# Portions of projection work dealt out anew between eight attention head pairs, with three pairs' closing transposes on other PSUM tiles

## The chip, the cores and the metric

The kernel runs on one NeuronCore of a Trainium2 chip. TensorE (PE) multiplies matrices and writes its results to PSUM; VectorE (DVE) and ScalarE (ACT) read PSUM, do the elementwise work and write to SBUF; GpSimd (POOL) does small elementwise work out of SBUF; SyncE (SP) issues most of the DMA transfers. Each engine works through its own list of instructions in order, and semaphores hold an instruction back until what it needs is there.

The metric is the device time in microseconds (us) of one launch of the whole program. The time before is the median of three runs, 1453.44 us (1450.69 to 1454.27). All times of single steps come from one profiled execution.

## The reference

One inference step of a two-layer encoder for 512 prompt frames and 8 running streams of 16 new frames, all in float32, model width 1024, 16 heads of 64. Layer 0 is a convolution module with an FFN. Then one K and one V are projected, and layer 1 projects queries and attends. Cut to the attention part, which is where the change lies:

```
k, v = split(rms_norm(h, norm_kv) @ w_kv, 2)
q = (rms_norm(h, norm_attn) @ w_q)             # 16 heads of 64
s = einsum("bqhd,bkhd->bhqk", q, k) * Dh**-0.5 + bias
p = softmax(where(valid, s, -1e30))
o = einsum("bhqk,bkhd->bqhd", p, v)
h = h + o @ w_o
h = h + (silu(a) * b) @ w_out                  # a, b from rms_norm(h) @ w_in
```

The prompt attends to itself in chunks of 64 frames, the running streams attend to 512 cached rows of K and V beside their own 16. A learned bias by head and clipped distance is added.

## The kernel before, in words

Activations lie with the feature on the partitions: `h` is 128 x 8 x 640, where 640 columns are 128 sample frames and 512 prompt frames. A float32 product is made of three fast matmuls: each operand is split into a high and a low part (ACT rounds the high part, DVE subtracts it to get the low part), and high x high, low x high and high x low are summed in PSUM. Splitting weights and activations is the main work of ACT and DVE.

The program has three stretches: layer 0, the attention, and the FFN of layer 1 with the final norm. The attention goes over eight pairs of heads, `p` = 0 to 7. Two kinds of work are woven into one PE order there:

- **Pair steps**, small and full of waits. `A` (`heads`, `head_a`): the prompt's scores, 24 matmuls, then bias, maximum, exp and scale on DVE and ACT. `s0`, `s1` (`samp_a`): scores of the running streams, two halves. `b00` to `b12` (`head_b`): transposes of the prompt's softmax rows, for two heads in three portions. `t0`, `t1` (`samp_b`): transposes of the streams' rows; `n0`, `n1` (its `rest`): one more transpose each, of the columns of the new frames, which DVE copies into `PM` and `PN`. `c0`, `c1` (`samp_c`): the streams' products with V, which DVE then scales into `Sn` and `Ss` (L1522). `P` (`pair_c`): the prompt's product with V, split by `osplit` into `oT[p]`. `d0`, `d1` (the `rest` of `samp_c`, L1524): one transpose each of the scaled rows and two `osplit`s of its halves.
- **Filler** (`stream`): the projections that the next pairs need, cut into portions of a few matmuls, in the order of `SETS`: `k` sets (K and Q of one pair, 12 portions), `v` sets (V of two pairs, 15 portions) and `o` sets (the output projection of two pairs, 16 portions, `set_o`). k1 and v1 come in pair 0, k2 in pair 1, and so on; o2 is the last. Each set also emits the splitting of the next set's weights (`pieces`), tied by `behind` to the last softmax instructions noted in `past`.

`BO[p]` is the order of pair p written out: a letter for a step, `f4` for four portions of filler, `f*` for what is left of the pair's portions. `FILL[p]` is the number of portions that pair p takes. Every PE instruction of a step is issued behind the one before (`pe`, `step_end`), so PE's order is exactly this text: if a step waits, PE waits. The steps have high priority over all later work; within that, the tile framework fixes each engine's order by its own simulated timeline. An instruction that comes early in ACT's or DVE's list is done first even if something more urgent becomes ready behind it.

PSUM has eight banks, three pools of tiles here: two `w2` tiles of two banks each (`w2t`: scores of `A`, of `s0` and `s1`, and, if `spare_w2[0]` is set, two portions of an `o` set side by side, evacuated by one wide add, L1361), two `am` tiles of one bank (`amt`: the last part of the scores in `A`, and the steps b, t, n, c, P and d) and two `mm` tiles of one bank (`mmt`: the filler). A tile can be written again when its readers are done. `spare_w2[0]` is cleared at `A` and set right after `s1`; `set_o` takes a `w2` tile for an even portion while more than two portions of the pair are left.

After pair 7 come `halves(3)`: the last quarter of the output projection, whose weights are split by `wsplit` (L178 on ACT, L183 on DVE, 128 x 2048 in one instruction each) as soon as the weight tile of the set two before it is free, which is at the end of k7, in pair 6. It takes `mm` and `am` tiles in turn and needs `oT[6]` and `oT[7]` whole. Then layer 1's FFN starts, with PE as the busy engine.

Of the kernel before, what the change touches and what calls it, by code (L numbers as in the profile page):

```python
# [15 lines left out]
P = 128  # L16
# [5 lines left out]
NP = H // 2  # L22
# [40 lines left out]
HIX = {X11: 0, X21: 1, XT1: 2, XT2: 3, XT3: 4, X22: 5, XT4: 6}  # L63
QORD = """50' a0 a1 10' 50" 10" 20 60' 30' 51' 60" 30" 51" 70 11 21 40 61 31 52 71 12 22 41 62 32 53 72
          13 23 42 63 33"""
BO = ["A f4 s0 s1 f3 b00 f1 b01 f1 b02 f1 b10 f1 b11 f1 b12 f1 t0 f1 t1 f1 n0 f1 n1 f1 c0 c1 P f1 d0 f1 d1 f*"] * 8
BO[1] = BO[6] = "A f4 s0 s1 f3 b00 f1 b01 b02 f1 b10 f1 b11 b12 f1 t0 t1 f1 n0 n1 c0 c1 P d0 d1 f*"
BO[7] = "A f2 s0 s1 f5 b00 f1 b01 b02 f1 b10 f1 b11 b12 f1 t0 f1 t1 n0 n1 f1 c0 c1 P d0 f1 d1 f*"
FILL = 27, 12, 28, 27, 28, 27, 12, 16
SETS = "k1 v1 k2 k3 o0 k4 v2 k5 o1 k6 v3 k7 o2"  # L70
LAG = 1
SSQ1 = 'aaaaaaaa'
# [13 lines left out]
def tile_trunk(ctx, tc, xT, vecs, hist, w_pw1, w_pw2, w_in0, w_out0, w_os0, w_in1, w_out1, w_os1,  # L86
# [17 lines left out]
    def nm(s):  # L104
        uid[0] += 1
        return f"{s}_{uid[0]}"
# [1017 lines left out]
    def amt():  # L1124
        return am.tile([P, 512], F32, tag="am", name=nm("am"))
# [29 lines left out]
    def bias_load(p):  # L1155
        for hh in range(2):
            hd = 2 * p + hh
            nc.sync.dma_start(BP[:, hh, 256:512],
                              bass.AP(tensor=rel.tensor, offset=rel.offset + hd * L + 127,
                                      ap=[[RELW - 1, P], [1, 256]]))  # L1160
            nc.gpsimd.tensor_scalar(out=BP[:, hh, 256:512], in0=BP[:, hh, 256:512],
                                    scalar1=t256[:, hd:hd + 1], scalar2=8.0,
                                    op0=ALU.subtract, op1=ALU.mult)
            nc.gpsimd.memset(BP[0:64, hh, 448:512], NEG)
        bt = ap.tile([P, 160], F32, tag="bt", name=nm("bt"), bufs=1)
        for b in range(4):
            nc.sync.dma_start(bt[b * 32:(b + 1) * 32, 0:128],
                              bass.AP(tensor=rel.tensor, offset=rel.offset + 2 * p * L + 127,
                                      ap=[[L, 2], [RELW - 1, 16], [1, 128]]))
            nc.sync.dma_start(bt[b * 32:(b + 1) * 32, 128:144],  # L1170
                              bass.AP(tensor=rel.tensor, offset=rel.offset + 2 * p * L + 255,
                                      ap=[[L, 2], [RELW - 1, 16], [1, 16]]))
        nc.gpsimd.tensor_scalar(out=BS[:, 384:512], in0=bt[:, 0:128], scalar1=ts_[:, p:p + 1],
                                scalar2=8.0, op0=ALU.subtract, op1=ALU.mult)
        for b in range(4):
            nc.gpsimd.tensor_scalar(out=BS[b * 32:(b + 1) * 32, 512 + b * 16:528 + b * 16],
                                    in0=bt[b * 32:(b + 1) * 32, 128:144],
                                    scalar1=ts_[b * 32:(b + 1) * 32, p:p + 1],
                                    scalar2=8.0, op0=ALU.subtract, op1=ALU.mult)
# [26 lines left out]
    fill, step_end, spare_w2 = None, [None], [None, []]  # L1206
    ahead, past, left = {}, [{}] * LAG, [0]

    def note(ins):
        ahead[ins.ins.engine] = ins.ins  # L1210
        return ins

    def osplit(src, hi, lo):
        note(xsplit(src, hi, lo))
        ahead[split_end[0].engine] = split_end[0]
# [47 lines left out]
    @contextmanager  # L1263
    def pe():
        with tc.issue_after(step_end[0]) if step_end[0] else nullcontext():
            yield
# [134 lines left out]
    def heads(ts):  # L1401
        KH, KL, QH, QL = ts
        wide = [w2t(), w2t()]
        narrow = [amt(), amt()]
        pss = [[], []]
        for i in ORD:
            n = (i + 1) * P
            o = SOFF[i]
            q = slice(i * P, (i + 1) * P)
            for hh in range(2):  # L1410
                pss[hh].append(narrow[hh][:, 0:n] if i == 1 else wide[hh][:, o:o + n])
            for j, (a, b) in enumerate(((QH, KH), (QL, KH), (QH, KL))):
                for hh in range(2):
                    r = slice(hh * DH, hh * DH + DH)
                    with pe():
                        step_end[0] = nc.tensor.matmul(pss[hh][-1], a[r, q], b[r, 0:n],
                                                       start=j == 0, stop=j == 2).ins
        return pss
# [47 lines left out]
    def samp_load(p, u):  # L1466
        cache = []
        for src in (kc[p, u], vc[p, u].rearrange("p b k d -> p b (k d)")):
            for i in range(2):
                t = ap.tile([P, 2, 512], F32, tag="cache", name=nm("cache"), bufs=CB)  # L1470
                nc.sync.dma_start(t, src[:, 2 * i:2 * i + 2, :])
                cache.append(t)
        return cache[:2], cache[2:]
# [35 lines left out]
    def samp_c(p, u, PTs, S, rs, VC):  # L1509
        v0 = 64 * u  # L1510
        PT, pn = PTs
        VT = vts[p // 2]
        pv = amt()
        for k in range(5):
            for b in range(4):
                c = slice(k * P + 32 * b, k * P + 32 * b + 32)
                step_end[0] = nc.tensor.matmul(
                    pv[32 * b:32 * b + 32, 0:P], PT[:, c] if k < 4 else pn[:, 32 * b:32 * b + 32],
                    VC[b // 2][:, b % 2, k * P:(k + 1) * P] if k < 4
                    else VT[:, 0, (p % 2) * P:(p % 2) * P + P], start=k == 0, stop=k == 4).ins  # L1520
        os_ = S[:, 0:P]
        note(nc.vector.tensor_scalar(out=os_, in0=pv[:, 0:P], scalar1=rs[:, 0:1], scalar2=None,  # L1522
                                     op0=ALU.mult))
        def rest():  # L1524
            tr = amt()
            step_end[0] = nc.tensor.transpose(tr[:, 0:P], os_, ident).ins
            trv = tr[:, 0:P].rearrange("p (b h q) -> p b h q", b=4, h=2)
            for hh in range(2):
                r = slice(hh * DH, hh * DH + DH)
                osplit(trv[r, :, hh, :],  # L1530
                       oT[p][0][r, v0:v0 + 64].rearrange("p (b q) -> p b q", q=SB),
                       oT[p][1][r, v0:v0 + 64].rearrange("p (b q) -> p b q", q=SB))

        return rest
# [24 lines left out]
    for p in range(NP):  # L1559
        if p < NP - 1:  # L1560
            oT[p] = (op_.tile([P, NT], F32R, tag="ohi", name=nm("ohi"), bufs=3),
                     op_.tile([P, NT], F32R, tag="olo", name=nm("olo"), bufs=3))
        else:
            oT[p] = (op_.tile([P, NT], F32, tag="kt", name=nm("ohi"), bufs=2).bitcast(F32R),
                     op_.tile([P, NT], F32, tag="qt", name=nm("olo"), bufs=QB).bitcast(F32R))
        ha, sa, pt, ps, left[0] = {}, {}, {}, {}, FILL[p]
        cache = [samp_load(p, u) for u in range(2)]
        for op in BO[p].split():
            if op[0] == "f":
                for _ in range(left[0] if op[1] == "*" else min(left[0], int(op[1]))):  # L1570
                    with pe():
                        next(fill)
                    left[0] -= 1
                    past.append(dict(ahead))
                continue
            past.append(dict(ahead))
            i = int(op[1]) if len(op) > 1 else None
            with pe(), tc.high_priority(offset=HP):
                if op[0] == "A":
                    assert not spare_w2[1]  # L1580
                    spare_w2[0] = False
                    pss = heads(split[p])
                    ha = {hh: head_a(p, hh, pss[hh]) for hh in range(2)}
                    pt = {hh: sp.tile([P, 1280], F32, tag="PT", name=nm("PT")) for hh in range(2)}
                elif op[0] == "s":
                    sa[i] = samp_a(p, i, w2t(), *cache[i])
                elif op[0] == "b":
                    head_b(ha[i], pt[i], int(op[2]))
                elif op[0] == "t":
                    ps[i] = samp_b(i, sa[i][0])  # L1590
                elif op[0] == "n":
                    ps[i] = ps[i]()
                elif op[0] == "c":
                    ps[i] = samp_c(p, i, ps[i], *sa[i])
                elif op[0] == "d":
                    ps[i]()
                else:
                    pair_c(p, (pt[0], pt[1]))
            if op == "s1":
                spare_w2[0] = True  # L1600
                if p + 1 < NP:
                    bias_load(p + 1)

    next(fill, None)
    adds = []
# [228 lines left out]
```

## Time and profile before

| what | value |
|---|---|
| median of three runs | 1453.44 us |
| profiled execution: its own time | 1452.18 us |
| profiled execution: span from first to last instruction | 1450.3 us |
| mean granted TensorE clock | 0.999 |
| attention, first pair's `A` to last pair's `d1` | 694.92 to 992.64 us |
| pair 1, `A` of pair 1 to `A` of pair 2 | 739.19 to 768.68 us |
| pair 6, `A` of pair 6 to `A` of pair 7 | 933.89 to 965.13 us |

The page gives busy times by engine, the span in 40 slices, the chain that ended last and the costliest groups of instructions; the trace behind it can be asked for the instructions of a stretch in order of time, for who waited for whom, and for the busy time in given stretches. A row of the timeline reads: start, length, engine, line, operation, tile written and tiles read, shapes, count, and in brackets how long the engine was idle before and what ended that. A matmul's length is modelled and matmuls overlap, so for PE the distance from one start to the next says more than the length.

### The profile page before, as it was taken

The numbers are of one execution on the slowest core, as the hardware profiler recorded it, in microseconds if no ns is written. First come the engines' busy times: TensorE is split into PE (matmuls) and PEld (weight loads), VectorE is DVE, ScalarE is ACT, GpSimd is POOL, SyncE is SP. The second block draws the span as 40 slices with busy tenths as digits, with TensorE's granted clock in tenths as the row PEclk, the third lists the DMA queues.
The fourth block names the chain that finished last, engine by engine and source line by source line (L and its number), as shares of the span: only waits on it lengthen the run. The fifth ranks groups of instructions, "written<-read, shape, count | busy, mean of one in ns | idle before, by whom it ended". The sixth has DMA issues, their size and how long they took to land. (4 is left out here: it accounts for less than half of the span.)

```text
span 1450.3 us, 28244 instructions
## 1 busy us (share of the span) xinstructions
PE 1420.6 (98%) x11086; PEld 1365.9 (94%) x11086; DVE 1119.6 (77%) x2489; ACT 749.7 (52%) x1633; POOL 283.0 (20%) x335
## 2 busy tenths in 40 slices
PE   9999999999999999999999999989999999999998
PEld 8998799999999999999988998978998999999998
DVE  6789867998788789765666757577898888888855
ACT  4666554564564464544654454443664464555443
POOL 5689121011111111012111111020011111111101
PEclk9999999999999999999999999999999999999999
DMA  7267424054544445424455555562035535444512
GB/s 245 73 174 192 130 80 145 12 142 122 145 110 135 131 115 128 136 88 171 163 182 196 190 176 180 166 211 73 30 90 137 148 108 136 128 118 120 153 60 73
DMA packets 66933, 192.58 MB, mean 133 GB/s; under 512 B 12144, under 2 KB 30320, under 8 KB 58480
## 3 DMA queue, kind: packets, MB, share of 16 engines
q1 hardware_dynamic: 52432, 160.58, 34.0%
q0 software_dynamic: 13504, 29.37, 10.2%
q8 instruction: 87, 1.43, 0.4%
q10 hardware_dynamic: 864, 0.83, 0.2%
q14 instruction: 46, 0.38, 0.1%
HBM read 179.14 MB, written 11.61 MB: 132 GB/s over the span
## 5 line engine op out<-in xcount | busy, mean ns | idle before, releaser
L442 PE MATMUL mm<-XH,whi 128*128 128x320 f32 x896 | 275.8, 310 | 3.7 <-ACT t L454 2.6
L442 PE MATMUL mm<-XH,wlo 128*128 128x320 f32 x896 | 276.1, 309 | 0.0
L442 PE MATMUL mm<-XL,whi 128*128 128x320 f32 x896 | 274.5, 309 | 0.0
L374 ACT ACTIVATE whi<-raw 128x512 fp32r<-128x512 f32 (+2 forms) x280 | 168.6, 613 | 136.5 <-PE mm L442 104.2
L375 DVE TENSOR_TENSOR wlo<-raw,whi 128x512 fp32r<-128x512 f32 (+2 forms) x280 | 184.5, 668 | 18.4 <-ACT whi L374 17.3
L442 PE MATMUL mm<-hid,whi 128*128 128x320 f32 x732 | 171.7, 310 | 3.0 <-DVE hid L375 2.2
L442 PEld LDWEIGHTS mm<-XH,whi 128*128 128x128 f32 x896 | 167.8, 188 | 5.5 <-ACT t L454 4.2
L442 PEld LDWEIGHTS mm<-XH,wlo 128*128 128x128 f32 x896 | 168.2, 188 | 0.0
L442 PEld LDWEIGHTS mm<-XL,whi 128*128 128x128 f32 x896 | 167.7, 188 | 0.0
L442 PEld LDWEIGHTS mm<-hid,whi 128*128 128x128 f32 x732 | 124.9, 188 | 5.5 <-DVE hid L375 3.2
L202 PE MATMUL mm<-xh,whi 128*128 128x320 f32 (+2 forms) x416 | 129.1, 312 | 0.4 <-DVE h L705 0.4
L203 PE MATMUL mm<-xh,wlo 128*128 128x320 f32 (+2 forms) x416 | 128.0, 309 | 0.0
L204 PE MATMUL mm<-xl,whi 128*128 128x320 f32 (+2 forms) x416 | 125.9, 310 | 0.9 <-DVE xl L192 0.9
L442 PE MATMUL mm<-hid,wlo 128*128 128x320 f32 x366 | 113.0, 309 | 0.0
L442 PE MATMUL mm<-XH,shi 128*128 128x320 f32 x344 | 105.9, 309 | 0.7 <-DVE h L1548 0.7
L442 PE MATMUL mm<-XH,slo 128*128 128x320 f32 x344 | 106.0, 308 | 0.0
L442 PE MATMUL mm<-XL,shi 128*128 128x320 f32 x344 | 105.5, 308 | 0.0
L420 POOL DMA_DIRECT2D s<-in_w_in x38 | 22.1, 583 | 376.1 <-DVE wlo L375 150.5
L844 POOL TENSOR_TENSOR ca<-ca,cvt 128x512 f32<-128x512 f32 x60 | 92.0, 1533 | 17.7 <-ACT cvt L841 11.2
L374 ACT ACTIVATE shi<-raw 128x512 fp32r<-128x512 f32 (+1 forms) x114 | 66.7, 588 | 43.5 <-PE mm L442 39.0
L583 DVE TENSOR_TENSOR h<-h,mm 128x320 f32<-128x320 f32 x168 | 79.9, 481 | 4.3 <-PE mm L442 4.1
L454 ACT ACTIVATE t<-mm 128x320 f32<-128x320 f32 x114 | 49.5, 434 | 60.9 <-PE mm L442 60.7
(331 smaller groups left out, 3698.0 us busy)
## 6 DMA issues: line engine op xcount, KB each, us to landing
raw<-in_w_in SPq DMA_DIRECT2D x38, 1024.0 KB
s<-in_w_in POOLq DMA_DIRECT2D x76, 256.0 KB, 4.1
raw<-in_w_os SPq DMA_DIRECT2D x24, 768.0 KB
cache<-in_ck SPq DMA_DIRECT2D x32, 512.0 KB
cache<-in_cv SPq DMA_DIRECT2D x32, 512.0 KB
raw<-in_w_pw SPq DMA_DIRECT2D x11, 1024.0 KB
s<-in_w_os POOLq DMA_DIRECT2D x48, 192.0 KB, 3.6
raw<-in_w_kq SPq DMA_DIRECT2D x8, 1024.0 KB
```

The lines of the kernel that those rows point to most:

```text
L202: nc.tensor.matmul(ps, wh, xh, start=(first and i == 0), stop=False)
L203: nc.tensor.matmul(ps, wl, xh, start=False, stop=False)
L204: end = nc.tensor.matmul(ps, wh, xl, start=False, stop=(stop and i == last))
L374: put_end[1] = nc.scalar.activation(out=hi, in_=src, func=AF.Copy).ins
L375: put_end[0] = nc.vector.tensor_tensor(out=lo, in0=src, in1=hi.bitcast(F32), op=sub).ins
L420: nc.gpsimd.dma_start(s1, src[:, 2 * n:3 * n])
L442: last = nc.tensor.matmul(pt, wt, v, start=(first and k == i == 0), stop=(k == n - 1 and i == 2), skip_group_check=True)
L454: keeps.append(nc.scalar.activation(out=t, in_=pt, func=AF.Copy).ins)
L583: nc.vector.tensor_tensor(out=hv, in0=hv, in1=pt, op=sub if row else add)
L844: nc.gpsimd.tensor_tensor(out=acc, in0=acc, in1=pr, op=ALU.add)
```

## The change

Only the order is changed: no instruction that computes is added or removed.

- `FILL`: pairs 0 and 5 take 20 portions instead of 27, pairs 1 and 6 take 19 instead of 12. The sum stays 177. So the last seven portions of v1 are made in pair 1 ahead of k2, and the last seven of v3 in pair 6 ahead of k7. Pairs 0 and 5 keep their text, so their `f*` after `d1` shrinks from 8 portions to 1.
- `BO[1]`, `BO[6]`: the seven portions go into places where two steps stood together (`b01 b02`, `b11 b12`, `t0 t1`, `n0 n1`) and ahead of `b00` and others; as before, none stands between `n1` and the end of the pair.
- `e0`, `e1` in pairs 1, 6 and 7 are `d0`, `d1` with their tile from the `mm` pool instead of the `am` pool.
- `w` is a step of its own that sets `spare_w2[0]`; `s1` no longer does. In pair 7 two more portions of o2 come between `s1` and `w`, and so use `mm` tiles. In the others `w` stands right behind `s1`; it adds one more snapshot to `past`.
- Pair 7 also moves one portion from between `n1` and `c0` to ahead of `n0`, and closes with `P f1 e0 e1 f*` instead of `P d0 f1 d1 f*`.

```diff
-BO = ["A f4 s0 s1 f3 b00 f1 b01 f1 b02 f1 b10 f1 b11 f1 b12 f1 t0 f1 t1 f1 n0 f1 n1 f1 c0 c1 P f1 d0 f1 d1 f*"] * 8
-BO[1] = BO[6] = "A f4 s0 s1 f3 b00 f1 b01 b02 f1 b10 f1 b11 b12 f1 t0 t1 f1 n0 n1 c0 c1 P d0 d1 f*"
-BO[7] = "A f2 s0 s1 f5 b00 f1 b01 b02 f1 b10 f1 b11 b12 f1 t0 f1 t1 n0 n1 f1 c0 c1 P d0 f1 d1 f*"
-FILL = 27, 12, 28, 27, 28, 27, 12, 16
+BO = ["A f4 s0 s1 w f3 b00 f1 b01 f1 b02 f1 b10 f1 b11 f1 b12 f1 t0 f1 t1 f1 n0 f1 n1 f1 c0 c1 P f1 d0 f1 d1 f*"] * 8
+BO[1] = BO[6] = "A f4 s0 s1 w f4 b00 f2 b01 f1 b02 f1 b10 f1 b11 f1 b12 f2 t0 f1 t1 f1 n0 f1 n1 c0 c1 P e0 e1"
+BO[7] = "A f2 s0 s1 f2 w f3 b00 f1 b01 b02 f1 b10 f1 b11 b12 f1 t0 f1 t1 f1 n0 n1 c0 c1 P f1 e0 e1 f*"
+FILL = 20, 19, 28, 27, 28, 20, 19, 16
...
-        def rest():
-            tr = amt()
+        def rest(tile):
+            tr = tile()
...
+            if op == "w":
+                spare_w2[0] = True
+                continue
...
-                elif op[0] == "d":
-                    ps[i]()
+                elif op[0] in "de":
+                    ps[i](amt if op[0] == "d" else mmt)
...
-            if op == "s1":
-                spare_w2[0] = True
-                if p + 1 < NP:
-                    bias_load(p + 1)
+            if op == "s1" and p + 1 < NP:
+                bias_load(p + 1)
```

## Prediction, made before the changed kernel was run

> **What bounds the kernel now.** I read the page's busy times first, then who PE waited for, pair by pair, then the timeline of the stretches with waits.
>
> ```profile
> span 1450.3 us, 28244 instructions
> ...
> PE 1420.6 (98%) x11086; PEld 1365.9 (94%) x11086; DVE 1119.6 (77%) x2489; ACT 749.7 (52%) x1633; POOL 283.0 (20%) x335
> ```
>
> PE is idle for 29.7 us of 1450.3. No matmul is removed, so only such idle time, and the refill behind it, can be won. PE's own waits from `b00` of pair 1 to the end of the pair:
>
> ```profile
> PE am L1526 <- DVE olo L192: 1.2, 1, 1.2
> PE am L1517 <- DVE PM L1503: 0.5, 1, 0.5
> PE am L1445 <- ACT PT L1449: 0.2, 1, 0.2
> ```
>
> In pair 6:
>
> ```profile
> PE am L1461 <- DVE Sn L1522: 2.1, 1, 2.1
> PE am L1526 <- DVE olo L192: 1.2, 1, 1.2
> PE am L1517 <- DVE PM L1503: 0.6, 1, 0.6
> ```
>
> In pair 7, behind `s1`, and later from `n0` on:
>
> ```profile
> PE w L1272 <- DVE mx L1202: 0.8, 1, 0.8
> ```
>
> ```profile
> PE am L1501 <- ACT PTs L1506: 0.6, 1, 0.6
> PE am L1526 <- DVE olo L192: 0.4, 1, 0.4
> ```
>
> The reader is to see that all but one of these name an `am` tile (that of pair 7's start a wide `w2` tile) whose reader on DVE or ACT is not done, that they stand in exactly the three pairs whose text the change rewrites, and that they come to 1.9, 3.9 and 1.8 us. Elsewhere PE is whole, as in this stretch of pairs 3 and 4 (length, then PE's busy time):
>
> ```profile
> 840.00:880.00 40.00, 40.00 (x387) 36.72 (x383) 24.27 (x78) 19.71 (x58) 6.57 (x11) 1.00 0.57 188
> ```
>
> Idle time is not the whole price. These PE rows are of pair 0 (undisturbed) and pair 6:
>
> ```profile
> 724.81 1.08 PE L1517 MATMUL am<-cache,PTs 128*32 128x128 f32 x32
> ...
> 727.13 2.37 PE L1461 MATMUL am<-PT,vt 128*64 128x512 f32 x16
> ```
>
> ```profile
> 955.71 0.27 PE L1501 MATMUL am<-ident,Ss 128*128 128x128 f32 x1
> 956.61 1.08 PE L1517 MATMUL am<-cache,PTs 128*32 128x128 f32 x32 [0.63 <-DVE PM L1503]
> ...
> 961.08 2.37 PE L1461 MATMUL am<-PT,vt 128*64 128x512 f32 x16 [2.08 <-DVE Sn L1522]
> 963.38 0.33 PE L1526 MATMUL am<-ident,Sn 128*128 128x128 f32 x1
> 964.88 0.33 PE L1526 MATMUL am<-ident,Ss 128*128 128x128 f32 x1 [1.16 <-DVE olo L192]
> ```
>
> From `c0` to `P` it is 2.32 us in pair 0 and 4.47 in pair 6: 2.15 lost. `d0` to `d1` takes 1.50; undisturbed a lone transpose takes 0.09 (991.07 to 991.16, below): 1.41 lost. `n1` to `c0` takes 0.90 against some 0.15: 0.75. So pair 6 loses 4.3 us, idle time plus 0.07 to 0.25 of refill at each stop. Pair 1, with 0.25, 0.2 and 0.2 put on its idle 1.2, 0.5 and 0.2, loses 2.5. Pair 7 loses about 0.8, 0.75 and 0.5.
>
> **The change, part by part.**
>
> *Pair 1.* One portion between `n0` and `n1`, and between `b11` and `b12`, gives DVE and ACT 1 to 1.7 us to read the `am` tile that the next step needs, so the waits for `PT` and `PM` go. `e0`, `e1` need no `am` tile, so `e1` no longer waits for the split of `P`; their `mm` tiles were read about 4 us earlier, under `c0`, `c1` and `P`. What is late next is `Sn` for `P`: behind the last portion DVE has the scaling of `qt`, `PN` and the low part of Q before it. I take 0.15 (0 to 0.4). Gain 2.5 - 0.15 = **2.35**, bounds 1.6 to 2.5. Splitting a joined pair of steps by filler costs nothing that shows: an extra matmul switch is below 0.1 us by the 0.09 of the lone transpose, and I count 0.
>
> *Pair 6.* The same, but for one long instruction:
>
> ```profile
> 957.75 2.29 DVE L183 TENSOR_TENSOR wlo<-raw,whi 128x2048 fp32r<-128x2048 f32 x1 [0.86 <-ACT whi L178]
> 959.96 0.69 DVE L1397 TENSOR_TENSOR QL<-qt,QH 128x512 fp32r<-128x512 f32 x1
> 960.67 0.35 DVE L1522 TENSOR_SCALAR Sn<-am,rs 128x128 f32<-128x128 f32 x1
> 960.94 0.34 DVE L1522 TENSOR_SCALAR Ss<-am,rs 128x128 f32<-128x128 f32 x1
> ```
>
> ```profile
> 955.80 1.91 ACT L178 ACTIVATE whi<-raw 128x2048 fp32r<-128x2048 f32 x1 [0.42 <-PE mm L1272]
> ```
>
> The split of the last output weights starts when k7 ends, and DVE's 2.29 us of it came just ahead of `Sn`, for which `P` waited. k7 still ends one transpose before `c0`. Count from k7's end (955.6): L178 is done at 2.1 as before, but `c0` now starts at 0.13 instead of 1.0, so `Sn` is ready at about 1.5, ahead of L183. In an order made by readiness `Sn` goes first and `P` doesn't wait. Then L183 fills DVE from 2.1 to 4.4, the low part of Q goes to 5.0 and `Ss` to 5.3; `P` ends at 4.75 and `e1`, which needs `Ss`, starts at 5.5 instead of 4.85. I take 0.65 for this new wait (0.1 if `Ss` comes before Q). Behind `e1` stands `A` of pair 7. Gain 4.3 - 0.65 = **3.65**. If DVE keeps L183 ahead of `Sn`, `P` waits until 5.4 instead of 2.45, and the gain is 4.3 - 3.0 = 1.3.
>
> *Pair 7, start.* The two portions on `mm` tiles take the place of the wait behind `s1`; their tiles are those of the two portions before `s0`, read by then. Gain **0.8** (0.5 to 0.8).
>
> *Pair 7, `n0` to `c0`.* The portion before `n0` covers the read of `t1`'s tile, but nothing now stands between `n1` and `c0`, which waits for `PM` as in pair 6 before, here with DVE free: about 0.4 instead of 0.75. Gain **0.35** (0 to 0.75).
>
> *Pair 7, end.* Before:
>
> ```profile
> 991.07 0.33 PE L1526 MATMUL am<-ident,Sn 128*128 128x128 f32 x1
> 991.16 0.40 PE L1272 MATMUL w<-ohi,whi 128*128 128x320 f32 x1
> ...
> 992.64 0.33 PE L1526 MATMUL am<-ident,Ss 128*128 128x128 f32 x1 [0.36 <-DVE olo L192]
> ```
>
> ```profile
> 991.19 0.70 ACT L190 ACTIVATE ohi<-am 128x512 fp32r<-128x512 f32 x2 [5.93 <-PE am L1461]
> 992.74 0.48 ACT L190 ACTIVATE ohi<-am 64x64 fp32r<-64x64 f32 x2 [0.85 <-DVE olo L192]
> ```
>
> ```profile
> 991.89 0.81 DVE L192 TENSOR_TENSOR olo<-am,ohi 128x512 fp32r<-128x512 f32 x2 [2.63 <-ACT ohi L190]
> 992.63 0.81 DVE L1361 TENSOR_TENSOR h<-w,h 128x640 f32<-128x640 f32 x1
> 993.47 0.48 DVE L192 TENSOR_TENSOR olo<-am,ohi 64x64 fp32r<-64x64 f32 x2
> ```
>
> The last two portions take `mm` tiles, and there are two. Now `e0` and `e1` take both just before them, so the portion behind `e1` waits until `e0`'s tile is read: ACT, DVE, ACT, DVE in turn, about 0.25 each. Count from `P`'s end: one portion (1.48 from 991.16 to 992.64, less the 0.5 lost) to 0.98, `e0`, `e1`, and the next portion could start at 1.16. `e0`'s first ACT part runs at 1.3 to 1.55; DVE then has the wide add (0.8) from 1.35 to 2.1, and the chain ends at 2.85. The portion starts at 3.0: 1.85 lost instead of 0.5. Cost **1.35** (0.3 if DVE takes the small parts first and nothing comes between). The third and fourth step are not hidden by anything: PE's order is fixed.
>
> The row at 992.74 shows ACT's second half idle for 0.85 until DVE had read the first. [...]
>
> *Pairs 0 and 5* lose seven portions behind `d1`. One is left, and `A`'s first scores go to `w2` tiles, so `d1`'s four splits (1.1 us by the same chain) are hidden under that portion. The next pair's K and V loads lose cover too:
>
> ```profile
> 725.90:734.50 8.60, 8.60 (x106) 7.16 (x99) 3.66 (x12) 3.88 (x12) 0.00 (x0) 1.00 0.77 246
> ```
>
> ```profile
> 731.47 0.36 PE L1272 MATMUL mm<-whi,xh 128*128 128x256 f32 x1
> ```
>
> ```profile
> 745.43 1.06 PE L1479 MATMUL w<-cache,qbd 128*32 128x512 f32 x8
> ```
>
> Between the first row's times the four loads of pair 1 move 2.1 MB at 246 GB/s. Pair 0's eight last portions run from 731.47 to `A` of pair 1 at 739.19; seven of them gone make some 7 us. `s0` of pair 1 came at 745.4 and will come at 738.4: 3.9 left. Cost 0, up to 4 if another 1 MB of weights gets ahead of them. The `out_v` and `out_k` transfers move with their portions and nobody waits for them. `w` and the extra snapshot in `past` only shift a few weight splits by an exp or two, seven portions before they are needed: 0.
>
> **Sum:** 2.35 + 3.65 + 0.8 + 0.35 - 1.35 = 5.8 us. The profiled execution took 1452.18 us (span 1450.3 and 1.9 around it) and would take 1446.4; on the scale of the median, 1453.44, it is **1447.6**. What follows the attention is carried by PE, so it moves up whole.
>
> **The rivals.**
>
> *L183 stays ahead of `Sn`.* For it: in pair 6 before the two became ready within 0.3 us of each other, and the order is fixed by a simulated time that I don't see. Against: `c0` moves 0.85 earlier. Saving 2.35 + 1.3 - 0.2 = 3.45: 1450.0.
>
> *Both new waits vanish too:* `Ss` before Q, and small splits before the wide add. Saving 2.35 + 4.2 + 1.15 - 0.3 = 7.4: 1446.0.
>
> *The `mm` tiles come free late (slower).* The first portion of pairs 2 and 7 wants `e0`'s tile, about 2.35 us after the end of `P`.
>
> ```profile
> 967.06 0.69 DVE L1202 CUSTOM_DVE_ANT_0 S<-w,BP 128x512 f32<-128x512 f32 x1 [0.84 <-PE w L1416]
> ```
>
> DVE's eight maximum steps of the next pair start 1.9 us after `A` begins, and run 3.6 us. If `e0`'s last DVE part stands behind them, that portion waits 3.9 us in both pairs: 7.7 lost, more than the 5.8 won, giving 1455.4. It decides whether `e0`'s last subtract (2.15 after `P` by the chain) comes before the first maximum (2.3). Against it: the steps of `e0` are older, and in pair 6 before DVE was idle 0.84 before that row.
>
> *It does not do what it says:* new waits in other places eat the gain, and the time stays near 1453.
>
> **How the numbers follow.** Forecast 0.56; both waits vanish 0.14; L183 ahead 0.15; no gain 0.08; late tiles 0.07. A measurement of this kernel can tell about 0.3% (4.4 us) from no change, so faster means below 1449.1: most of the first (it has 1.3 us of room) and all of the second give 0.60. Same: L183 ahead, no gain, late tiles by themselves (2 us above before), and the upper end of the forecast, 0.34. Slower 0.06: late tiles where L183 is ahead as well (2.35 more, 1457.8) or the cache loads are late. The range takes in the second rival with its bounds (1444.0) and L183 ahead and no gain (1453.0).
>
> **What would show it.** PE's waits for `am` in pairs 1 and 6 gone but for some 0.1 to 0.7 us at `P` or `e1`; `P` of pair 6 within 2.5 us of `c0`; L183 behind `Sn`; no PE wait behind `s1` in pair 7; a new wait of 1 to 2 us of a portion on an `mm` tile, for `olo`, behind the last `e1`. The time from pair 0's `A` to the first portion of `halves(3)` should shrink by 5 to 7 us and nothing behind it change. I am wrong if L183 precedes `Sn`, if portions of pairs 2 or 7 wait for `mm`, or if `s0` waits for the cache loads.

## The result, and the profile after

| | time of a launch, us | profiled execution, us | its span, us |
|---|---|---|---|
| before | 1452.53 median of 6 runs (1449.69 to 1454.27) | 1452.18 | 1450.3 |
| after | 1445.01 median of 6 runs (1444.48 to 1445.45) | 1445.22 | 1443.4 |

The ratio is 0.995, with a 95% interval of 0.9938 to 0.9963: the change makes the kernel faster by 0.4 to 0.6%. The prediction, 1447.6 us in a range of 1444.0 to 1453.0, holds.

The page of the changed kernel shows that the same work is done in less idle time:

```profile
span 1443.4 us, 28243 instructions
...
PE 1420.6 (98%) x11086; PEld 1366.8 (95%) x11086; DVE 1118.9 (78%) x2490; ACT 748.6 (52%) x1633; POOL 284.3 (20%) x335
```

PE is busy for 1420.6 us as before, and its idle time falls from 29.7 to 22.8 us. Who PE waited for, from 690 to 1005 us (releaser, us in total, times, longest):

```profile
PE w L1623 <- DVE sqs L1616: 1.5, 1, 1.5
PE am L202 <- ACT ohi L190: 0.5, 1, 0.5
PE am L1445 <- ACT PT L1449: 0.3, 1, 0.3
PE am L1517 <- DVE PM L1503: 0.3, 1, 0.3
PE w L257 <- POOL sqs L1627: 0.3, 1, 0.3
PE mm L1526 <- DVE Ss L1522: 0.3, 1, 0.3
```

In pair 1 no wait is left at all, in pair 6 only the last of these rows. The third and the fourth are of pair 7 and the others lie behind it. For two of the rows behind pair 7 the kernel before has to be looked at as well. Its view has a wait for the sums of squares there, and none at L202:

```profile
PE w L1622 <- DVE sqs L1615: 1.0, 1, 1.0
```

So the wait for the sums has grown by 0.5 us and a new one of 0.5 stands ahead of it. To see what this comes to, cut the timeline at the starts of PE's first `A` row of each pair (L1416), at the end of the last `P` (L1461; taken as the start of PE's first row behind it), and at the first matmul of the FFN (L442). Between such marks lie these times, in us:

| stretch | before | after | difference | predicted |
|---|---|---|---|---|
| start to `A` of pair 0 | 694.92 | 694.46 | -0.46 | 0 |
| pairs 0 and 1 | 73.76 | 71.38 | -2.38 | -2.35 |
| pairs 2 to 4 | 123.79 | 123.79 | 0 | 0 |
| pairs 5 and 6 | 72.67 | 68.90 | -3.77 | -3.65 |
| `A` of pair 7 to the end of its `P` | 25.93 | 25.01 | -0.92 | -1.15 |
| end of `P` to the first FFN matmul | 20.77 | 21.58 | +0.81 | +1.35 |
| FFN to the end | 438.48 | 438.26 | -0.22 | 0 |
| span | 1450.32 | 1443.38 | -6.94 | -5.8 |

The five stretches that the change touches, or lies between, give -6.26; the other 0.68 stands ahead of the first changed instruction and in the FFN, and is looked at last. Here is pair 6 of the changed kernel as PE ran it (start, length, engine, line, operation, tiles, shapes; in brackets the idle time before and its releaser):

```profile
953.06 1.08 PE L1517 MATMUL am<-cache,PTs 128*32 128x128 f32 x32
...
955.38 2.37 PE L1461 MATMUL am<-PT,vt 128*64 128x512 f32 x16
957.69 0.33 PE L1526 MATMUL mm<-ident,Sn 128*128 128x128 f32 x1
958.27 0.33 PE L1526 MATMUL mm<-ident,Ss 128*128 128x128 f32 x1 [0.25 <-DVE Ss L1522]
958.52 0.50 PE L1416 MATMUL w<-KH,QH 64*128 64x512 f32 x2
```

and DVE beside it:

```profile
954.43 0.35 DVE L1522 TENSOR_SCALAR Sn<-am,rs 128x128 f32<-128x128 f32 x1 [0.48 <-PE am L1517]
955.05 2.29 DVE L183 TENSOR_TENSOR wlo<-raw,whi 128x2048 fp32r<-128x2048 f32 x1 [0.27 <-ACT whi L178]
957.26 0.69 DVE L1397 TENSOR_TENSOR QL<-qt,QH 128x512 fp32r<-128x512 f32 x1
957.87 0.35 DVE L1522 TENSOR_SCALAR Ss<-am,rs 128x128 f32<-128x128 f32 x1
```

From `c0` to `P` it is 2.32 us (955.38 less 953.06), as in an undisturbed pair, where it was 4.47: the scaling of `Sn` is now the first of the four DVE rows and the long split L183 the second. `Ss` is the last of them, and `e1` waits for it: 0.58 from `e0` to `e1` against 0.11 without a wait (984.52 to 984.63, below), so 0.47 lost. This is the new wait that the prediction put there, at 0.65.

And the end of pair 7, PE of the changed kernel:

```profile
984.52 0.27 PE L1526 MATMUL mm<-ident,Sn 128*128 128x128 f32 x1
984.63 0.27 PE L1526 MATMUL mm<-ident,Ss 128*128 128x128 f32 x1
984.66 0.39 PE L202 MATMUL am<-ohi,whi 128*128 128x320 f32 x1
...
986.33 0.41 PE L202 MATMUL am<-ohi,whi 128*128 128x320 f32 x1 [0.53 <-ACT ohi L190]
...
987.02 0.31 PE L1272 MATMUL mm<-ohi,whi 128*128 128x320 f32 x1
...
999.54 0.83 PE L1623 MATMUL w<-onec,sqs 128*128 128x1 f32 x6 [1.51 <-DVE sqs L1616]
```

Here is a thing that the prediction had excluded. Behind `e1` stand not the last two portions (L1272, from 987.02) but ten matmuls of `halves(3)` (L202 to L204). `halves` is not issued inside `pe`, so nothing ties its matmuls behind `step_end`, and the framework put them into the gap. PE stood idle for 0.53 us there instead of the 1.85 that were forecast to be lost. Whether that is why the stretch lost 0.81 and not 1.35 is what the second set of experiments asks.

### The profile page after: what moved, and what is told of

It reads as the page before. It is cut to its first block, busy times and chain, and to the rows that moved or that the text cites. A ratio compares the mean times of both kernels' runs of the same rounds, so it can differ in the third digit from the quotient of the medians.

```text
span 1443.4 us, 28243 instructions
## 1 busy us (share of the span) xinstructions
PE 1420.6 (98%) x11086; PEld 1366.8 (95%) x11086; DVE 1118.9 (78%) x2490; ACT 748.6 (52%) x1633; POOL 284.3 (20%) x335
## 5 line engine op out<-in xcount | busy, mean ns | idle before, releaser
L442 PE MATMUL mm<-XH,whi 128*128 128x320 f32 x896 | 275.9, 310 | 2.6 <-ACT t L454 2.6
L442 PE MATMUL mm<-XH,wlo 128*128 128x320 f32 x896 | 276.3, 309 | 0.0
L442 PE MATMUL mm<-XL,whi 128*128 128x320 f32 x896 | 274.6, 309 | 0.0
L442 PE MATMUL mm<-hid,whi 128*128 128x320 f32 x732 | 172.0, 310 | 3.7 <-DVE hid L375 2.7
L442 PEld LDWEIGHTS mm<-XH,whi 128*128 128x128 f32 x896 | 167.8, 188 | 4.2 <-ACT t L454 4.2
L442 PEld LDWEIGHTS mm<-XH,wlo 128*128 128x128 f32 x896 | 168.2, 188 | 0.0
L442 PEld LDWEIGHTS mm<-XL,whi 128*128 128x128 f32 x896 | 167.7, 188 | 0.0
L442 PEld LDWEIGHTS mm<-hid,whi 128*128 128x128 f32 x732 | 124.9, 188 | 6.4 <-DVE hid L375 3.7
L202 PE MATMUL mm<-xh,whi 128*128 128x320 f32 (+2 forms) x416 | 129.3, 313 | 1.0 <-ACT xh L190 0.6
L204 PE MATMUL mm<-xl,whi 128*128 128x320 f32 (+2 forms) x416 | 126.0, 310 | 0.0
L442 PE MATMUL mm<-hid,wlo 128*128 128x320 f32 x366 | 113.0, 309 | 0.0
L442 PE MATMUL mm<-XH,shi 128*128 128x320 f32 x344 | 106.0, 309 | 0.7 <-DVE h L1548 0.7
L442 PE MATMUL mm<-XH,slo 128*128 128x320 f32 x344 | 106.0, 308 | 0.0
L442 PE MATMUL mm<-XL,shi 128*128 128x320 f32 x344 | 105.5, 308 | 0.0
```

Of the source, the lines that this page charges most:

```text
L202: nc.tensor.matmul(ps, wh, xh, start=(first and i == 0), stop=False)
L204: end = nc.tensor.matmul(ps, wh, xl, start=False, stop=(stop and i == last))
L442: last = nc.tensor.matmul(pt, wt, v, start=(first and k == i == 0), stop=(k == n - 1 and i == 2), skip_group_check=True)
```

## The experiments

All kernels of one set ran on the same chip, beside runs of the kernel before on it (the first row has those of the three sets; the second row is the change beside its own runs of before, as above). The last two columns are cut from each one's timeline as above (`A` of pair 0 to the first FFN matmul; end of the last `P` to the same). Where nothing was changed and the clock did not fall, such times repeat to some 0.05 us from kernel to kernel; the times of launches scatter by 1 to 6 us.

| kernel | median, us (runs) | ratio to before, 95% interval | `A` of pair 0 to FFN | end of `P` to FFN |
|---|---|---|---|---|
| before | 1449.77 (26), 1451.15 (9), 1450.61 (9) | | 316.92 | 20.77 |
| after | 1445.01 (6) | 0.995 (0.9938 to 0.9963) | 310.66 | 21.58 |
| after, second time | 1445.69 (5) | 0.9962 (0.995 to 0.9975) | 311.60 | 22.60 |
| deal_only | 1447.03 (8) | 0.9978 (0.9968 to 0.9988) | 313.88 | 20.77 |
| close_only | 1447.59 (11) | 0.9984 (0.9976 to 0.9993) | 314.29 | 20.77 |
| late_split_before | 1448.90 (12) | 0.9993 (0.9984 to 1.0002) | 316.61 | 20.77 |
| p7_close_d | 1441.97 (5) | 0.9942 (0.993 to 0.9954) | 309.81 | 20.77 |
| p7_old | 1443.42 (4) | 0.9949 (0.9934 to 0.9964) | 310.71 | 20.77 |
| tied_halves | 1442.53 (4) | 0.9946 (0.9931 to 0.9961) | 310.30 | 21.25 |
| p7_later_b | 1443.94 (5) | 0.9952 (0.9939 to 0.9964) | 311.53 | 21.74 |
| sums_pool | 1443.15 (5) | 0.9945 (0.9931 to 0.9958) | 309.02 | 19.89 |
| tied_sums_pool | 1443.78 (4) | 0.9952 (0.9939 to 0.9966) | 310.24 | 21.25 |
| sums_pool_c | 1442.85 (4) | 0.9943 (0.9929 to 0.9956) | 309.47 | 19.89 |
| late_split_after | 1445.98 (1) | | 311.60 | 21.58 |

### First set: which edit does what

**deal_only**: the kernel before, with the portions dealt as in the change in pairs 0, 1, 5 and 6, but all closing transposes on `am` tiles and pair 7 untouched.

```diff
-BO[1] = BO[6] = "A f4 s0 s1 f3 b00 f1 b01 b02 f1 b10 f1 b11 b12 f1 t0 t1 f1 n0 n1 c0 c1 P d0 d1 f*"
+BO[1] = BO[6] = "A f4 s0 s1 f4 b00 f2 b01 f1 b02 f1 b10 f1 b11 f1 b12 f2 t0 f1 t1 f1 n0 f1 n1 c0 c1 P d0 d1"
-FILL = 27, 12, 28, 27, 28, 27, 12, 16
+FILL = 20, 19, 28, 27, 28, 20, 19, 16
```

> The kernel before with only the seven portions dealt to pairs 1 and 6 and put between their steps; the closings stay d0 d1 on am tiles, pair 7 and the point at which wide tiles are freed stay as before. Theory (each stop is its own price): the waits for PT, PM and Sn go, the d0-d1 wait of 1.4 us stays in both pairs: pair 0's A to pair 2's A shrinks by 1.0 us, pair 5's A to pair 7's A by 2.9 us, the time by 3.9 us. Rival (the dealing does it all, since the closings merely wait for what the dealing makes early): the d0-d1 wait goes too and the time falls by 6 us. Rival (the closings do it all): no fall.

Measured: pairs 0 and 1 take 1.00 less, pairs 5 and 6 take 2.85 less. The kernel's waits:

```profile
PE am L1526 <- DVE olo L192: 2.1, 3, 1.2
...
PE am L1445 <- ACT PT L1449: 0.6, 1, 0.6
...
PE am L1526 <- DVE Ss L1522: 0.5, 1, 0.5
```

The wait of `P` for `Sn` is gone without any change to the closings, the closing waits for `olo` stay (1.2 in pair 1, 0.6 in pair 6, 0.4 in pair 7), and pair 6 waits for `Ss` as well, as `e1` does in the change. The second row was not expected: it is `b01` of pair 2, a pair that takes 0.83 longer here, so that the whole stretch wins 3.04 and not the 3.9 expected. ACT's copy of `PT` (at 781.06) stands behind the exps of `s0` and `s1` (at 778.42 and 779.55), and the first of those had waited 2.26 for DVE. In the changed kernel no such row stands in pair 2. I did not follow it further.

**close_only**: the kernel before, with `e0 e1` for `d0 d1` in pairs 1 and 6 alone.

```diff
-BO[1] = BO[6] = "A f4 s0 s1 f3 b00 f1 b01 b02 f1 b10 f1 b11 b12 f1 t0 t1 f1 n0 n1 c0 c1 P d0 d1 f*"
+BO[1] = BO[6] = "A f4 s0 s1 f3 b00 f1 b01 b02 f1 b10 f1 b11 b12 f1 t0 t1 f1 n0 n1 c0 c1 P e0 e1 f*"
```

> The kernel before with only the closing transposes of pairs 1 and 6 on mm tiles (e0 e1), portions dealt as before. Theory: the d0-d1 wait of 1.4 us goes in both pairs and nothing else: time lower by 2.8 us; P of pair 6 still waits 2.1 us for Sn. Rival (the tile is not the point, the split of P would be waited for by the next A anyway): the wait moves to the last scores of the next A and the time falls by less than 1 us.

Measured: pair 1 1.20 and pair 6 1.39 less, and `P` of pair 6 waits on:

```profile
PE am L1461 <- DVE Sn L1522: 2.1, 1, 2.1
```

So the two edits mend different waits. Alone they win 3.04 and 2.63, together 5.67; the change has 6.15 in pairs 0, 1, 5 and 6. Two effects of opposite sign make most of the difference: pair 2's 0.83 comes only with the first, and in pair 6 the wait for `Ss` (0.47) is left when both other waits have gone. Pair 1 wins some 0.2 more from both together than from the two alone, which was not followed.

**late_split_before**: the kernel before, with the split of the last output weights (1.91 us on ACT, 2.29 on DVE) tied behind `b02` of pair 7.

```diff
+    tie6 = []
...
-        wh, wl = wsplit(w_o[r], 16, P)
+        wh, wl = wsplit(w_o[r], 16, P, ties=tuple(tie6))
...
+            if p == 7 and op == "b02":
+                tie6[:] = ahead.values()
```

> The kernel before with only the split of the last output weights (1.9 us on ACT, 2.3 us on DVE) moved from pair 6's end to behind b02 of pair 7. Theory (that split is what P of pair 6 waited for): P follows c0 within 2.4 us, the wait of 2.1 us for Sn is gone and nothing takes its place: pair 6's A to pair 7's A falls by 2.1 us and the time by 2 us. Rival (Sn is late for another reason, the low part of Q): the wait at P falls by less than 1 us. Rival (its place in pair 7 costs as much): pair 7 grows by 1 to 2 us.

Measured: pair 6 takes 2.14 less, so the split was the cause of `P`'s wait; the part of it that stood ahead of `Sn` on DVE is L183, as the prediction read it. But pair 7 takes 1.83 more, with two new waits:

```profile
PE w L1272 <- DVE mx L1202: 1.5, 2, 0.8
...
PE am L1495 <- DVE PT L1451: 0.8, 1, 0.8
```

The second row is `t0`, for a copy that stands behind L183 on DVE. The first row has the wait that the kernel before has there too and a new one of 0.76, at 972.31 us. That one is not a wait behind the split, whose first instruction starts at 976.19: three scalings of the prompt's rows (L1432, from 970.57) now stand between the maxima of `s0` and `s1` on DVE, which in the kernel before follow each other. Tying the split changed DVE's order ahead of it as well, so not all of the 1.83 is the price of its new place.

**late_split_after** (third set) did the same to the changed kernel:

> The changed kernel with the split of the last output weights (1.91 on ACT, 2.29 on DVE) tied behind `b02` of pair 7. Theory (this split is what `e1` of pair 6 still waits behind): `e1`'s wait for `Ss` goes, pair 6 from 33.96 to 33.5. Rival, expected as well from late_split_before: its new place in pair 7 costs some 1.8 there, so the whole is slower by 1 to 1.5 us; if DVE and ACT have room in the new pair 7, the whole is 0.5 faster.

Measured: pair 6 is 0.40 shorter and `e1`'s wait is gone; pair 7 is 1.37 longer, 1.3 of it one wait of `t0` for the copy that stands behind the split on DVE:

```profile
PE am L1495 <- DVE PT L1451: 1.3, 1, 1.3
```

The whole stretch is 0.94 longer. The rival is borne out: of these two places the new one is the worse. What the dealing did for `P` is therefore not to remove the 2.29 us, but to let the short `Sn` go ahead of them.

### Second set: what the end of pair 7 costs, and why

**p7_close_d** (run in the first set): the change, with pair 7 closing on `am` tiles as before.

```diff
-BO[7] = "A f2 s0 s1 f2 w f3 b00 f1 b01 b02 f1 b10 f1 b11 b12 f1 t0 f1 t1 f1 n0 n1 c0 c1 P f1 e0 e1 f*"
+BO[7] = "A f2 s0 s1 f2 w f3 b00 f1 b01 b02 f1 b10 f1 b11 b12 f1 t0 f1 t1 f1 n0 n1 c0 c1 P d0 f1 d1 f*"
```

> The changed kernel with pair 7's closing put back to am tiles and to the order P d0 f1 d1 f*; the rest of pair 7 as changed. Theory (the closing of pair 7 on mm tiles costs, as the trace shows 0.8 us more from the end of P to the first matmul of the FFN): time 0.8 us below the changed kernel. Rival (from P's end to the FFN the sum of squares on DVE sets the pace): the same time as the changed kernel within 0.3 us, with the wait for the sums longer by what PE saves.

Measured: 20.77 again from the end of `P`, 0.81 less than the change, as the theory has it. Its PE rows there:

```profile
979.58 2.38 PE L1461 MATMUL am<-PT,vt 128*64 128x512 f32 x16
...
983.45 0.33 PE L1526 MATMUL am<-ident,Ss 128*128 128x128 f32 x1 [0.35 <-DVE olo L192]
...
997.08 0.83 PE L1623 MATMUL w<-onec,sqs 128*128 128x1 f32 x6 [0.98 <-DVE sqs L1616]
```

**tied_halves**: the change, with the matmuls of `halves` put inside `pe`, so that none can go ahead of the last two portions.

```diff
-                half_end[0] = mm3(
+                with pe():
+                    half_end[0] = mm3(
...
```

> The changed kernel with the matmuls of the last quarter of the output projection tied into PE's order behind the portions, so that none of them can be put ahead of the last two portions of o2. Theory (the prediction's 1.35 for the end of pair 7 came out as 0.8 only because ten such matmuls filled the wait for the two `mm` tiles): PE waits 1.0 to 1.9 us behind `e1` for an `mm` tile, from the end of `P` to the first FFN matmul takes 22.2 to 23.0 instead of 21.6, time 0.6 to 1.4 us over the changed kernel: 1445.6 to 1446.4. Rival (the sums of squares on DVE set the end of that stretch, whatever fills the wait): 21.6 as before, the longer wait behind `e1` is taken back at the wait for the sums, and the time is that of the changed kernel within 0.3 us.

Measured: 21.25, and here are PE's rows:

```profile
981.29 0.42 PE L1272 MATMUL w<-ohi,whi 128*128 128x320 f32 x1
...
982.38 0.27 PE L1526 MATMUL mm<-ident,Ss 128*128 128x128 f32 x1
984.32 0.38 PE L1272 MATMUL mm<-ohi,whi 128*128 128x320 f32 x1 [1.67 <-DVE olo L192]
...
996.97 0.83 PE L1624 MATMUL w<-onec,sqs 128*128 128x1 f32 x6
```

The reader is to see two things. With the order fixed, the portion behind `e1` starts 3.03 us after the end of `P` (984.32 less 981.29; the prediction had 3.0), and 1.94 after `e1`, of which 0.09 is no loss: 1.85 lost, to the digit the forecast. Yet the stretch grows by 0.48 over the kernel before, not by 1.35, because the wait at the sums of squares, 0.98 in p7_close_d and 1.51 in the change, is all but gone (no bracket at 996.97). My theory falls: the matmuls put into the gap did not save the time, for without them the stretch is 0.33 shorter, not longer. Its rival was nearer: in the change the end of this stretch is set behind PE's waits, on DVE. There the first addition of `halves` and the last sum of squares stand like this, in p7_close_d,

```profile
987.19 0.49 DVE L1548 TENSOR_TENSOR h<-mm,h 128x320 f32<-128x320 f32 x1 [1.12 <-PE mm L204]
...
996.55 0.48 DVE L1616 TENSOR_TENSOR sqs<-sqs 128x320 f32<-128x320 f32 x1
```

in the change,

```profile
989.38 0.48 DVE L1548 TENSOR_TENSOR h<-am,h 128x320 f32<-128x320 f32 x1
...
998.48 1.01 DVE L1616 TENSOR_TENSOR sqs<-sqs 128x320 f32<-128x320 f32 x2
```

and in tied_halves:

```profile
987.23 0.49 DVE L1549 TENSOR_TENSOR h<-am,h 128x320 f32<-128x320 f32 x1 [0.39 <-PE am L204]
...
996.44 0.48 DVE L1617 TENSOR_TENSOR sqs<-sqs 128x320 f32<-128x320 f32 x1
```

The first addition comes 5.31, 5.85 and 5.94 us after the end of `P`, the start of the last sum (the second of the two that the change's last row groups) 14.66, 15.46 and 15.14. Between the two DVE has 9.2 to 9.6 us of additions, sums and weight splits. In tied_halves one addition fewer, 0.4, stands ahead of the last sum, eleven for twelve; by these rows that is why it ends sooner than the change though it began later.

**p7_old**: the change with the whole text of pair 7 as before.

```diff
-BO[7] = "A f2 s0 s1 f2 w f3 b00 f1 b01 b02 f1 b10 f1 b11 b12 f1 t0 f1 t1 f1 n0 n1 c0 c1 P f1 e0 e1 f*"
+BO[7] = "A f2 s0 s1 w f5 b00 f1 b01 b02 f1 b10 f1 b11 b12 f1 t0 f1 t1 n0 n1 f1 c0 c1 P d0 f1 d1 f*"
```

> The changed kernel with the whole text of pair 7 as it was before (`w` right behind `s1`, one portion between `n1` and `c0`, `d0 f1 d1`): only pairs 0, 1, 5 and 6 are changed. Theory (the three edits of pair 7 nearly cancel: the wait behind `s1` comes back, 0.8, and the wait at `n0`, against the 0.8 of the close and the new wait at `b02`): from `A` of pair 7 to the first FFN matmul 46.7 (46.4 to 47.0) against 46.6, time within 0.4 us of the changed kernel, 1445.1. Rival (the deal of portions in pairs 5 and 6 made pair 7 faster or slower than before, so that its text is worth more): more than 0.8 us away from the changed kernel.

Measured: 46.69 from `A` of pair 7 to the FFN, against 46.59 in the change. This is the theory's 46.7: the edits of pair 7 together are worth 0.10 us, since what the start wins, the end takes. The median is 1443.42, under the change's, but the intervals of the two ratios overlap.

**p7_later_b**: p7_close_d with `f4` for `f3` ahead of `b00`.

```diff
-BO[7] = "A f2 s0 s1 f2 w f3 b00 f1 b01 b02 f1 b10 f1 b11 b12 f1 t0 f1 t1 f1 n0 n1 c0 c1 P d0 f1 d1 f*"
+BO[7] = "A f2 s0 s1 f2 w f4 b00 f1 b01 b02 f1 b10 f1 b11 b12 f1 t0 f1 t1 f1 n0 n1 c0 c1 P d0 f1 d1 f*"
```

> The changed kernel with `d0 f1 d1` on `am` tiles at the end of pair 7 (as p7_close_d) and four portions instead of three ahead of `b00` in pair 7, so one fewer behind the last step. Theory (in pair 7 the exps on ACT set the pace of the first transposes; a portion more ahead of `b00` covers the wait of `b02` for the copy of `PT`): that wait of 0.3 to 0.5 goes, pair 7 to the end of `P` lasts one portion (about 1.5) less the wait longer and the stretch behind it one portion shorter; 0.5 us under p7_close_d, 1441.5. Rival (the wait is handed on to the next step, or the last steps lack the portion): equal to p7_close_d within 0.3 us, 1442.0, with a new wait behind `P`.

Measured: neither theory nor rival. Of its 21.74 behind `P`, 1.1 goes with a fall of the granted clock (0.66 from 1000 to 1005 us, where the change had 1.00): from PE's L257 rows to the FFN it takes 3.74 us instead of 2.61. Without it the stretch is 20.6, only 0.16 shorter for a portion less, while pair 7 up to the end of `P` is 0.76 longer. Its waits:

```profile
PE w L1623 <- DVE sqs L1616: 1.7, 1, 1.7
PE am L1517 <- DVE PM L1503: 0.9, 1, 0.9
```

The wait of `b02` went (0.3) and that of `c0` for `PM` grew from 0.3 to 0.9. Behind `P` PE lost at the sums what it had less to do. And the portion was mis-sized in my expectation: it is 0.88 us (two of them from 987.02 to 988.78 in the change); the 1.5 that I used had a wait in it. What this run shows is that time added ahead of `P` is paid in full here, while a portion less behind it wins little, as long as DVE sets the end.

**after, second time:**

> The changed kernel as it is, again, beside the three others on the same chip. Expected: 1445 us (1444.3 to 1445.6), ratio 0.995; pair 7 from its `A` to the end of `P` 25.0, from there to the first FFN matmul 21.6.

Measured: 24.99 and 22.60. The extra 1.02 lies between the matmuls of the sums and the L257 rows behind them (3.98 us instead of 2.96), where the clock fell again, in this view by stretches (length, busy us of PE, PEld, DVE, ACT and POOL, granted clock, DMA share, GB/s):

```profile
1000.00:1005.00 5.00, 5.00 (x28) 5.00 (x28) 3.77 (x6) 0.72 (x2) 1.56 (x1) 0.72 0.91 321
```

The waits ahead of it repeat to 0.1 us.

### Third set: DVE's cover taken off

**sums_pool**: p7_close_d, with three of the seven additions of squares on POOL, which is idle there (0.00 us busy from 980 to 995 us in p7_close_d).

```diff
-                sq_end = nc.vector.tensor_tensor(out=acc, in0=acc if k > 1 else sqs[:, 0:NH],
+                eng = nc.gpsimd if k < 4 else nc.vector
+                sq_end = eng.tensor_tensor(out=acc, in0=acc if k > 1 else sqs[:, 0:NH],
...
```

> p7_close_d with three of the seven additions of squares behind pair 7 (128 x 320, 0.40 us apart on DVE) moved from DVE to POOL, which stands idle there. Theory (DVE, not PE, sets the end of the stretch behind pair 7: in five kernels its last addition starts 14.66 us after the end of `P` and the first FFN matmul comes at 20.77, and PE waits 1.0 for it): DVE ends up to 1.2 earlier, PE's wait for the sums of squares shrinks from 1.0 to 0 to 0.2, from the end of `P` to the first FFN matmul 19.7 to 20.0. Rival (ACT's squares or PE's own order set it): 20.77 and the same wait.

**tied_sums_pool**: tied_halves with the same edit.

> tied_halves (`e0`, `e1` on `mm` tiles at the end of pair 7, nothing hoisted ahead of the last two portions) with the same three additions on POOL. Theory (the prediction's price for PE is right, 1.35 by 1.85 less 0.5, and only DVE's chain behind it hid most of it): with that cover taken off, 1.35 more than sums_pool from the end of `P` to the first FFN matmul, 21.0 to 21.3, no more than 0.25 under tied_halves (21.25), whereas sums_pool is 0.8 to 1.0 under p7_close_d. Rival (the mm tiles cost only about 0.5 by themselves): 0.5 more than sums_pool, 20.3.

Measured: 19.89 and 21.25, both as the theories have it. In sums_pool no wait for the sums is left:

```profile
980.66 2.37 PE L1461 MATMUL am<-PT,vt 128*64 128x512 f32 x16
...
997.27 0.83 PE L1624 MATMUL w<-onec,sqs 128*128 128x1 f32 x6
```

From the start of `P` to the matmuls of the sums it takes 16.61 us where p7_close_d took 17.50 (997.08 less 979.58), 0.89 less. With the same edit tied_halves stays at 21.25, since it had no DVE wait to lose; its PE rows in tied_sums_pool:

```profile
985.64 0.38 PE L1272 MATMUL mm<-ohi,whi 128*128 128x320 f32 x1 [1.66 <-DVE olo L192]
...
998.29 0.83 PE L1625 MATMUL w<-onec,sqs 128*128 128x1 f32 x6
```

Between the two kernels that differ only in how pair 7 closes and whether `halves` is tied, the distance is now 1.36 us, against 0.48 with all sums on DVE. That is the 1.35 of the prediction, and it shows where the other 0.88 had gone: under a wait for DVE that was there before the change. The change itself, with its untied `halves`, was not run with sums on POOL; that its 0.81 is DVE's lateness is read from its rows above.

**sums_pool_c**: sums_pool with one of the last two portions put between `n1` and `c0`.

```diff
-BO[7] = "A f2 s0 s1 f2 w f3 b00 f1 b01 b02 f1 b10 f1 b11 b12 f1 t0 f1 t1 f1 n0 n1 c0 c1 P d0 f1 d1 f*"
+BO[7] = "A f2 s0 s1 f2 w f3 b00 f1 b01 b02 f1 b10 f1 b11 b12 f1 t0 f1 t1 f1 n0 n1 f1 c0 c1 P d0 f1 d1 f*"
```

> sums_pool with one of the last two portions of pair 7 moved ahead, between `n1` and `c0`. Theory (with DVE's chain relieved PE sets the end, so covering the wait of `c0` for `PM` with a portion from behind is a gain now): from `A` of pair 7 to the first FFN matmul 0.2 to 0.5 less than sums_pool. Rival (DVE sets it still, so a portion moved ahead of `P` only pushes the end out, as p7_later_b's 0.6): 0.5 or more longer than sums_pool.

Measured: 45.42 from `A` of pair 7 to the FFN against 45.04, so 0.38 longer: between the two theories, nearer to the rival. The wait of `c0` is covered, but with a portion less behind `P`, PE meets DVE again at the sums:

```profile
PE w L1624 <- DVE sqs L1617: 1.0, 1, 1.0
```

So sums_pool had just brought the two engines level. Why DVE does not begin sooner when PE has a portion less to do I did not settle.

## Why the prediction was right, and where it was not

**Pairs 0 and 1** (2.35 predicted, 2.38 measured). The waits for `PT`, `PM` and `olo` went as read from the view of waits, idle time plus refill; the new wait of 0.15 at `P` did not come. close_only and deal_only give 1.20 and 1.00 of it singly. That pair 0's lost cover costs nothing also held: no wait of `s0` or of a portion for its tile stands in pair 1.

**Pairs 5 and 6** (3.65 predicted, 3.77 measured). The order on DVE is that of the forecast: `Sn`, L183, the low part of Q, `Ss`. The rival in which L183 stays ahead of `Sn` is refuted by the four DVE rows, and deal_only shows that the dealing, not the closing, turns the order. late_split_before shows the split to be the cause of the old wait. The new wait of `e1` was 0.47, not 0.65.

**Pair 7 up to `P`** (1.15 predicted, 0.92 measured). The wait behind `s1` went (0.8). `c0` starts 0.54 behind `n1`, idle for 0.3 of it, which by the text's 0.15 for an undisturbed step is the 0.4 forecast. Not foreseen was a wait of `b02`, 0.3 idle, for the copy of `PT`: `b01` and `b02` take 1.08 us here and 0.57 in p7_old. PE reaches this step sooner once it no longer stops behind `s1`, and the wait comes out there; p7_old, which keeps the stop, has no wait at `b02`. With 0.5 lost there the sum would be 0.65 and not 0.92. Most of the rest lies in portions of filler that are 0.1 to 0.15 us shorter than in p7_old, and why was not followed.

**Pair 7 from `P` on** (cost 1.35 predicted, 0.81 measured): this is the step that failed, though little hung on it. Its arithmetic was right, 1.85 us lost behind `e1` (tied_halves), and two of its statements were wrong. "PE's order is fixed" does not hold behind `e1`, where ten matmuls of `halves` went ahead, and the wait of 1 to 2 us for an `mm` tile that was to show there did not stand in the changed kernel. tied_halves shows that the filling cost 0.33 rather than saving anything; by the DVE rows, it put one addition more ahead of the last sum. "The third and fourth step are not hidden by anything", and "nothing behind it change", overlooked PE's wait of 1.0 for the sums of squares, which was in the trace of before: a loss of PE ahead of a wait for another engine is paid only as far as that engine is late too. In the change DVE is late too, by 0.80 at the last sum, and 0.81 is what was paid. With the wait for DVE taken away on both sides the price is 1.36.

In the kernel before, ACT's second half of a tile stood idle for 0.85 us until DVE had read the first (the row at 992.74 of the prediction). On `mm` tiles, in tied_halves, the order is the same:

```profile
982.58 0.33 ACT L190 ACTIVATE ohi<-mm 64x64 fp32r<-64x64 f32 x2 [0.57 <-PE mm L1526]
983.69 0.35 ACT L190 ACTIVATE ohi<-mm 64x64 fp32r<-64x64 f32 x2 [0.78 <-DVE olo L192]
```

The second halves of both tiles wait 0.78 for DVE, which begins to read the first ones at 983.45, and with this chain in it the closing cost 1.36. The rows tell how the kernel's instructions were ordered; an order with ACT's second half under DVE's first was not tried.

**The rival that ended slower**, `mm` tiles coming free late by 3.9 us in pairs 2 and 7, did not happen: no portion of pair 2 or of pair 7 up to `P` waits for an `mm` tile. What was to decide it is in DVE's rows at the start of pair 7 in the changed kernel, where the last subtracts of `e0` and `e1` come ahead of the first maximum:

```profile
959.53 0.37 DVE L192 TENSOR_TENSOR olo<-mm,ohi 64x64 fp32r<-64x64 f32 x2 [0.15 <-ACT ohi L190]
960.45 0.69 DVE L1202 CUSTOM_DVE_ANT_0 S<-w,BP 128x512 f32<-128x512 f32 x1 [0.55 <-PE w L1416]
```

**The level.** On the profiled execution the forecast was 1446.4 and the time 1445.22. Of these 1.2 us, 0.46 lie in the changed stretch (6.26 for 5.8), 0.46 ahead of the first changed instruction and 0.22 in the FFN; these two belong to single executions, as the last section shows. The medians fell by 7.5 us, more than the 6.26 that the cut of the timeline accounts for, and the rest can't be told from scatter. That the stretches come as near as 6.26 to 5.8 is in part luck, since two errors partly offset each other: the end of pair 7 cost 0.54 less than forecast, its start won 0.23 less.

**What it leaves.** The change's own best part is without pair 7's closing: p7_close_d is 0.8 us shorter from `A` to the FFN, and sums_pool 1.6. Both beat the kernel before by their intervals; that they beat the change is shown by the cut of the timeline and not by the times of launches, whose intervals overlap. Of sums_pool's further gain nothing shows in the launches (ratio 0.9945, p7_close_d 0.9942), and its profiled execution had the longest FFN of the fourteen, 438.9 us, where p7_close_d's had the shortest, 437.6. Up to 63 us into the FFN the two keep step to 0.02 us; the difference comes later.

## What to carry to other kernels

When a wait is added to the bounding engine, look along its queue for the next place where it waits for another engine anyway: up to that wait's length the new one is free, if the other engine's chain doesn't get later by it too, as it did in the change (0.80 at the last sum; in tied_halves 0.48 of 1.36 was paid, ahead of the place where p7_close_d waits 0.98). So that chain has to be worked out as well. A wait behind one long instruction on a helper engine can go by reaching the point a little sooner, so that the short instruction is ready first (in pair 6 `Sn`, 0.35 us, ahead of L183's 2.29); moving the long one elsewhere lost most of what it won, or more, in another pair (1.83 of 2.14 in the kernel before, 1.37 for 0.40 in the changed one). What is left untied in an order written out by hand can be moved into its gaps, as ten matmuls were here, and a filled gap isn't yet a gain.

## What the runs showed that was not expected

The time up to `A` of pair 0 ran from 690.93 to 694.92 us over the fourteen profiled executions, whose programs have the same text ahead of that point, and single falls of the granted clock go with a part of it. In the change's execution, with a clock of 0.87 and 64 PE instructions in 10 us,

```profile
30.00:40.00 10.00, 10.00 (x64) 10.00 (x63) 8.72 (x17) 3.82 (x9) 5.87 (x3) 0.87 0.28 108
```

in that of tied_halves, with 1.00 and 74:

```profile
30.00:40.00 10.00, 10.00 (x74) 10.00 (x73) 9.38 (x17) 3.86 (x9) 6.39 (x3) 1.00 0.22 84
```

The kernel before had 1.00 there too and yet the latest `A`, so the clock is not all of it, and the rest stays open. The stretch from the first FFN matmul to the end ran from 437.6 to 438.9 us. With launches of one kernel scattering by 1 to 6 us, gains of under 1 us, like those of the second and third set, could be told only from the timeline between two marks, where undisturbed executions repeat to some 0.05 us.
